# T and C of a state-space layer in one table, T's zero quarter not loaded, the input steps as outer partition index, and the transpositions put directly behind pv

## The chip, the cores and the metric

The kernel runs on one core of a Trainium2 chip. The metric is the device time of one launch in microseconds; of the kernel before, the median of three runs is 1155.27 us (1155.26 to 1155.54). The core has a matrix engine (TensorE, PE in the profile, its weight loads apart as PEld), a vector engine (VectorE, DVE), an activation engine (ScalarE, ACT), a general engine (GpSimd, POOL) and SyncE (SP), which in this kernel issues nearly all transfers. Every engine works through its own instructions in order and waits for others by semaphores. DMA engines carry the transfers.

## The reference

Two layers of width 1024 over 512 positions, float32. Layer 0 mixes with a stick-breaking attention, layer 1 with a complex diagonal state-space layer (SSM) and a GLU; each is followed by a gated MLP with a causal convolution of width 3, and everything is modulated by a vector c. The change concerns the SSM alone:

```python
def s5_ssm(h, w_in, a_re, a_im, log_dt, b_re, b_im, c_re, c_im, d_skip, w_glu, b_glu, w_o):
    u = h @ w_in
    ug = u.reshape(b, s, 64, 16)                     # 64 groups of 16 channels
    lam_bar = exp((a_re + 1j * a_im) * exp(log_dt)[:, None])   # 64 states a group
    b_bar = ((lam_bar - 1) / lam)[..., None] * (b_re + 1j * b_im)
    bu = einsum('gph,bsgh->bsgp', b_bar, ug)
    states = scan over s: x[s] = lam_bar * x[s - 1] + bu[s]
    y = einsum('ghp,bsgp->bsgh', c_re + 1j * c_im, states).real + d_skip * u
    z = gelu(y)
    return (z * sigmoid(z @ w_glu + b_glu)) @ w_o
```

## The kernel before, in words

Dense matrices are multiplied in three products of float32 halves (mm3, L170, L173, L174: high by high, high by low, low by high), each 128x128 against 128x512. A weight tile is loaded by SyncE (L162), its high half is made by ScalarE (L164) and its low half by VectorE (L165). In the background, wg tiles (L200, L201) carry the matrix-vector products with c.

The program runs in stages: attention, the first FFN (up and dn matmuls), the SSM, its GLU and output projection, the second FFN. The SSM's tables depend on weights alone, and they are made during the first FFN, from about 275 us of the profiled execution on, by ssm_prep.

**The tables.** The 64 groups are worked on in 8 blocks of 8 groups. The 512 positions are cut into 64 chunks of 8 steps. For each block there are four tables in device memory: B (input to the chunk's state contribution), R (rotations), T (the direct path, within a chunk, from 8 input steps x 16 channels to 8 output steps x 16 channels, for 8 groups) and C (from the chunk's starting state to the 8 output steps). T from input step j to output step i is zero where i < j.

**ssm_prep, per block.** GpSimd multiplies lam and bt (L1004 to L1009, called by cmul_in), with lam and bt loaded by load_bl (L1182, L1183; issued through held, which fixes SyncE's order and shows as L1173). SyncE stores lam to sB. GpSimd multiplies bc with powers to cl (L1232 to L1237). Then, for two blocks together (for block 7 alone), direct (L1161) lets TensorE multiply cl with bd to pk, from which ScalarE and VectorE write kz, a band of 112 zeros and 128 kernel values. t_out writes T out of kz: for input step j a window of 128 columns that begins at 112 - 16 j. cl_out writes C out of cl. The steps of ssm_prep are a generator whose pieces are put between the FFN's pieces, and its TensorE matmuls stand in the FFN's stream at places fixed by the program; held keeps the order of its transfers on SyncE, among weight loads.

**The SSM.** load_scan and load_out fetch B, R, T and C of a block, two blocks ahead. Per step s_, st_out(s_ - 2) multiplies u with T and the states with C into py (L1312 in the profile is the helper's line for py and pv; 8 matmuls each, shown as 16 of the trace's), st_scan(s_) multiplies u with B into pv and VectorE scans it; st_tr(s_ - 2) transposes yn, ScalarE's copy of py, into pz (L1396), and four gelus read pz. Dense glu matmuls fill TensorE between them: run(2) issues two of them between pv and the transpositions, run(100) the rest.

Of the kernel before, what the change touches and what calls it, by code (L numbers as in the profile page):

```python
# [8 lines left out]
F32 = mybir.dt.float32  # L9
# [8 lines left out]
P = 128  # L18
T = 512
D = 1024  # L20
KD = D // P
# [31 lines left out]
FINT = 1  # L53
FORD = (0, 1, 2, 3, 4, 5, 7, 6)
NGLU = 5
NU = 4
NPRE = 3
KPRE = 5
NWT = 6
# [26 lines left out]
def _trunk(ctx, tc, I, out, tap):  # L86
# [13 lines left out]
    dram = pool("dram", space=DRAM)  # L100
# [4 lines left out]
    def bank(p=None, name="ps"):  # L105
        p = p or mm
        return p.tile([P, 512], F32, tag="b", name=name)
# [32 lines left out]
    def follow(eng, fn):  # L140
        with tc.issue_after(line[eng].ins) if eng in line else ExitStack():
            line[eng] = fn()
        return line[eng]
# [837 lines left out]


    sB = dram.tile([8, P, 2, 512], F32, tag="sB", name="sB")
    sC = dram.tile([8, P, 8, P], F32, tag="sC", name="sC")
    sT = dram.tile([8, P, 8, P], F32, tag="sT", name="sT")
    sR = dram.tile([8, P, 2, 256], F32, tag="sR", name="sR")
    sL = dram.tile([2, 8, NPAIR * P], F32, tag="sL", name="sL")

# [2 lines left out]
    def ssm_prep(fc):  # L991
# [22 lines left out]
        def gen():  # L1014
# [152 lines left out]
            def t_out(bi, js):  # L1167
                kz = kza[:, bi % 2, :]
                for j in js:
                    held(sT[bi].rearrange("(h j) g c -> j g h c", j=8)[j], kz[:, 112 - 16 * j:240 - 16 * j])  # L1170

            def held(out, in_):
                tc.keep_in_program_order(SP.dma_start(out, in_))  # L1173


            def load_bl(bi):
                put = held if bi else G.dma_start
                lam = pb.tile([P, 2, 512], F32, tag="lam", name="lam")
                bt = pb.tile([P, 2, 512], F32, tag="bt", name="bt")
                cs = slice(bi * 512, (bi + 1) * 512)  # L1180
                for ri in range(2):
                    put(lam[:, ri, :], sL[ri, :, cs].rearrange("(o j) x -> o j x", o=1).to_broadcast([16, 8, 512]))  # L1182
                    put(bt[:, ri, :], I[("b_reT", "b_imT")[ri]][:, cs].rearrange("h (o x) -> h o x", o=1).to_broadcast([16, 8, 512]))  # L1183
                return lam, bt

            def cl_out(bi, cl):
                for ri in range(2):
                    for g2 in range(2):
                        held(sC[bi, ri * 64:ri * 64 + 64].rearrange("n (q g) c -> g n q c", g=2)[g2],
                             cl[g2 * 64:g2 * 64 + 64, ri, :, 1:, :].rearrange("n q a h -> n q (a h)"))  # L1190


# [78 lines left out]
    def ssm(R):  # L1271
# [3 lines left out]
        with ExitStack() as zc:  # L1275
# [3 lines left out]
            with ExitStack() as sc:  # L1279
                tp = sc.enter_context(tc.tile_pool(name="sst", bufs=1, reuse_waits="tile"))  # L1280

                def load_scan(bi):
# [3 lines left out]
                    for g, src in (("B", sB), ("R", sR)):  # L1286
                        follow("P", lambda: SP.dma_start(d[g].rearrange("p r n -> p (r n)"), src[bi].rearrange("p r n -> p (r n)")))

                def load_out(bi):
                    d = blk[bi]  # L1290
                    d["T"] = tp.tile([P, 8, P], F32, tag="pT", bufs=2, name="pT")
                    d["C"] = tp.tile([P, 8, P], F32, tag="pC", bufs=2, name="pC")
                    for g, src in (("T", sT), ("C", sC)):
                        follow("P", lambda: SP.dma_start(d[g].rearrange("p r n -> p (r n)"), src[bi].rearrange("p r n -> p (r n)")))

                for bi in range(2):
                    load_scan(bi)
# [9 lines left out]
                def run(n):  # L1307
                    for q in range(min(n, len(dense))):
                        dense.pop(0)()
# [5 lines left out]
                def u_out(bi, ps):  # L1315
                    d = blk[bi]
                    ut = sp.tile([P, CH, NC], F32, tag="ut", bufs=2, name="ut")
                    S.activation(ut, ps.rearrange("p (c j) -> p j c", j=CH), AF.Copy)
                    (S if bi < 4 else G).dma_start(sU[bi].rearrange("j p c -> p j c"), ut)
                    u = d["u"] = sp.tile([P, 8, NC], F32, tag="u", bufs=NU, name="u")  # L1320
                    pin["u"] = SP.dma_start(u.rearrange("p g c -> p (g c)"), sU[bi].rearrange("j (h g) c -> h j (g c)", g=8))

                for bi in range(4):
                    u_out(bi, hd[bi][1])
# [9 lines left out]
                def st_scan(bi):  # L1334
                    d = blk[bi]
                    u = d["u"]
                    rho = rhos[bi % 2]
                    S.activation(rho[:, :, 1:], decay[:, bi * 4:bi * 4 + 4].rearrange("p (q o) -> p q o", o=1).to_broadcast([P, 4, NC - 1]), AF.Copy)
                    pv = bank(aux, name=f"pv{bi}")
                    for q in range(4):  # L1340
                        for ri in range(2):
                            for g2 in range(2):
                                mm(pv[g2 * 64:g2 * 64 + 64, ri * 256 + q * 64:ri * 256 + q * 64 + 64],
                                   d["B"][:, ri, q * P + g2 * 64:q * P + g2 * 64 + 64], u[:, 2 * q + g2, :], start=True, stop=True)
                    R = d["R"]
                    v2 = pv.rearrange("p (r n) -> p r n", r=2)
                    cosb, sinb = (R[:, q:q + 1, :].to_broadcast([P, 2, 256]) for q in range(2))
                    rho = rho.rearrange("p q c -> p (q c)")

                    def tmp(tag, bufs=1):  # L1350
                        return sp.tile([P, 2, 256], F32, tag=tag, bufs=bufs, name=tag)

                    m1, m2, vr = tmp("m1", 2), tmp("m2"), tmp("vr")
                    V.tensor_tensor(m1, v2, cosb, ALU.mult)
                    V.tensor_tensor(m2, v2[:, ::-1, :], sinb, ALU.mult)
                    for ri in range(2):
                        V.tensor_tensor(m1[:, ri], m1[:, ri], m2[:, ri], (ALU.add, ALU.subtract)[ri])
                        V.tensor_tensor_scan(vr[:, ri], rho, m1[:, ri], 0.0, ALU.mult, ALU.add)
                    s1, s2 = tmp("m1", 2), tmp("m2")
                    V.tensor_tensor(s1, vr, cosb, ALU.mult)  # L1360
                    V.tensor_tensor(s2, vr[:, ::-1, :], sinb, ALU.mult)
                    for ri in range(2):
                        pin["comb"] = V.tensor_tensor(s1[:, ri], s1[:, ri], s2[:, ri], (ALU.subtract, ALU.add)[ri])

                    d["s1"] = s1
                    if not bi:
                        st_state(bi)
# [25 lines left out]
                def st_tr(bi):  # L1393
                    yn = blk[bi]["yn"]
                    for i in range(4):
                        pe_pin(PE.transpose(pz[:, i * P:(i + 1) * P], yn[:, 2 * i:2 * i + 2].rearrange("p i q h -> p (i q h)"), ident))  # L1396
                    for i in range(2):
                        for g2 in range(2):
                            S.activation(zf[bi][g2 * 64:g2 * 64 + 64].rearrange("p (a i c) -> p a i c", a=4, i=2)[:, :, i, :],
                                         pz[i * 64:i * 64 + 64].rearrange("p (a g c) -> p a g c", a=4, g=2)[:, :, g2, :], AF.Gelu_apprx_tanh)  # L1400
                    tap(f"z{bi}", zf[bi])
# [20 lines left out]
                def glu_w(mt):  # L1422
                    return load_w(I["w_glu"][(mt - NGLU) * P:(mt - NGLU + 1) * P, :], name=f"wgl{mt}")

# [9 lines left out]
                run(USTG[1])  # L1434
                pz = bank(name="pz")
                gb = None
                for s_ in range(2, 10):
                    st_out(s_ - 2)
                    if s_ < 8:
                        st_scan(s_)  # L1440
                    if s_ + 1 < 8:
                        load_scan(s_ + 1)
                    if s_ < 8:
                        load_out(s_)
                    if s_ > 2:
                        if s_ == 3:
                            zh = new_h()
                            gb = [bank(name=f"glu{mt}") for mt in range(NGLU)]
                        glu_units(s_ - 3)
                    run(2)  # L1450
                    st_tr(s_ - 2)
                    if s_ >= 8:
                        with behind_head([pin["low"], pin["comb"]]):
                            bg((1, 2)[s_ - 8], False)
                    run(100)

                gw, g5 = glu_w(NGLU), bank(aux, name=f"glu{NGLU}")
                for k in range(KD - 1):
                    mm3(g5, wk(gw, k), (zh[0][k], zh[1][k]), k == 0, False, True)
                glu_units(KD - 1)  # L1460
                run(100)
                mm3(g5, wk(gw, KD - 1), (zh[0][KD - 1], zh[1][KD - 1]), False, True, True)
                gb.append(g5)
            gp = zc.enter_context(tc.tile_pool(name="ssg", bufs=1, reuse_waits="tile"))
            gz = []
# [225 lines left out]
```

## Time and profile before

| | us |
|---|---|
| median of three runs | 1155.27 |
| profiled execution | 1157.38 |
| its span | 1155.6 |
| TensorE busy | 1145.3 (99%) |
| VectorE busy | 853.3 (74%) |
| ScalarE busy | 563.6 (49%) |
| GpSimd busy | 273.7 (24%) |

The profiled execution was 1157.38 us long, 2.1 us over the median; 1.8 us of it lie around the span. The mean granted TensorE clock is 0.998. Times of a timeline are us from the start of the span. An instruction's row gives its start, its length, engine, line, operation and tiles (out<-in), a count where several follow each other, and in brackets the idle time before it and what ended that. Matmuls overlap, so the distance of two starts is what a matmul costs, and less than its length.

### The profile page before, as it was taken

The numbers are of one execution on the slowest core, as the hardware profiler recorded it, in microseconds if no ns is written. First come the engines' busy times: TensorE is split into PE (matmuls) and PEld (weight loads), VectorE is DVE, ScalarE is ACT, GpSimd is POOL, SyncE is SP. The second block draws the span as 40 slices with busy tenths as digits, with TensorE's granted clock in tenths as the row PEclk, the third lists the DMA queues.
The fourth block names the chain that finished last, engine by engine and source line by source line (L and its number), as shares of the span: only waits on it lengthen the run. The fifth ranks groups of instructions, "written<-read, shape, count | busy, mean of one in ns | idle before, by whom it ended". The sixth has DMA issues, their size and how long they took to land.

```text
span 1155.6 us, 16407 instructions
## 1 busy us (share of the span) xinstructions
PE 1145.3 (99%) x6170; PEld 957.4 (83%) x6170; DVE 853.3 (74%) x1271; ACT 563.6 (49%) x894; POOL 273.7 (24%) x277
## 2 busy tenths in 40 slices
PE   9999999999999999999999999999999999999997
PEld 7888787798888888888889888899888888888887
DVE  7869989578987677777877688787886378744655
ACT  7656667456542244313446477547543144422443
POOL 1001010000678898779800000000000000000002
PEclk9999999999999999999999999999999999999999
DMA  9775564333367588697765797461366266332322
GB/s 345 282 264 162 183 201 147 126 92 110 94 207 245 157 267 247 192 311 251 233 219 192 225 333 278 167 201 56 110 218 200 73 159 207 126 111 75 93 69 73
DMA packets 87954, 211.00 MB, mean 183 GB/s; under 512 B 15554, under 2 KB 34114, under 8 KB 87875
## 3 DMA queue, kind: packets, MB, share of 16 engines
q1 hardware_dynamic: 79026, 192.39, 51.0%
q0 software_dynamic: 4544, 16.26, 4.3%
q10 hardware_dynamic: 4304, 1.31, 0.5%
q8 instruction: 48, 0.79, 0.3%
q14 instruction: 32, 0.25, 0.1%
HBM read 188.68 MB, written 21.24 MB: 182 GB/s over the span
## 4 chain that ended last, share of the span: by engine, by line
PE 92%; DMA 4%; DVE 2%; issue 1%; ACT 1%; SPq 0%; DVEq 0%
PE up L170 13%; PE up L173 13%; PE up L174 13%; PE dn L170 7%; PE dn L173 7%; PE dn L174 7%; PE up L333 4%; PE u L333 2%; PE o L838 1%; PE wo L170 1%; PE t L822 1%; PE wo L173 1%; PE wo L174 1%; PE wos L174 1%; PE wos L170 1%; PE wos L173 1%
## 5 line engine op out<-in xcount | busy, mean ns | idle before, releaser
L170 PE MATMUL up<-hH,up_h 128*128 128x512 f32 x640 | 249.6, 390 | 0.0
L173 PE MATMUL up<-hL,up_h 128*128 128x512 f32 x640 | 249.1, 389 | 0.0
L174 PE MATMUL up<-hH,up_l 128*128 128x512 f32 x640 | 249.0, 389 | 0.0
L461 DVE SCALAR_TENSOR_TENSOR ca<-up,small,ca 128x511 f32<-128x511 f32 (+1 forms) x176 | 131.6, 747 | 109.4 <-ACT ca L459 106.4
L170 PE MATMUL dn<-gH,dn_h 128*128 128x512 f32 (+1 forms) x394 | 144.5, 368 | 0.0
L173 PE MATMUL dn<-gL,dn_h 128*128 128x512 f32 (+1 forms) x394 | 144.4, 366 | 0.0
L174 PE MATMUL dn<-gH,dn_l 128*128 128x512 f32 (+1 forms) x394 | 144.3, 366 | 0.0
L170 PEld LDWEIGHTS up<-hH,up_h 128*128 128x128 f32 x640 | 120.1, 188 | 25.8 <-issue 0.4
L459 ACT ACTIVATE ca<-up,small 128x512 f32<-128x512 f32 x88 | 68.3, 776 | 149.3 <-PE up L174 143.2
L174 PEld LDWEIGHTS up<-hH,up_l 128*128 128x128 f32 x640 | 120.1, 188 | 25.0
L173 PEld LDWEIGHTS up<-hL,up_h 128*128 128x128 f32 x640 | 120.1, 188 | 24.7
L201 DVE SCALAR_TENSOR_TENSOR wg<-wg,cact 128x1024 f32<-128x1024 f32 x96 | 121.3, 1283 | 7.8 <-DMA wg<-in_w_modT_dram 7.7
L164 ACT ACTIVATE up_h<-up_r 128x1024 fp32r<-128x1024 f32 x80 | 84.2, 1052 | 83.2 <-PE dn L173 61.9
L165 DVE TENSOR_TENSOR up_l<-up_r,up_h 128x1024 fp32r<-128x1024 f32 x80 | 113.7, 1421 | 14.3 <-ACT up_h L164 13.4
L1554 POOL TENSOR_SCALAR xa<-x,Anorm_out 128x256 f32<-128x256 f32 x7 | 6.2, 881 | 461.4 <-DVE x L356 461.4
L356 DVE SCALAR_TENSOR_TENSOR x<-dn,mod,x 128x512 f32<-128x512 f32 (+1 forms) x55 | 37.4, 680 | 71.2 <-PE dn L174 71.2
L170 PEld LDWEIGHTS dn<-gH,dn_h 128*128 128x128 f32 x394 | 74.3, 189 | 12.4 <-issue 0.2
L173 PEld LDWEIGHTS dn<-gL,dn_h 128*128 128x128 f32 x394 | 74.3, 189 | 12.2
L174 PEld LDWEIGHTS dn<-gH,dn_l 128*128 128x128 f32 x394 | 74.3, 189 | 12.1
L164 ACT ACTIVATE dn_h<-dn_r 128x1024 fp32r<-128x1024 f32 (+1 forms) x48 | 46.5, 980 | 45.8 <-PE dn L173 40.8
L165 DVE TENSOR_TENSOR dn_l<-dn_r,dn_h 128x1024 fp32r<-128x1024 f32 (+1 forms) x48 | 61.3, 1278 | 2.4 <-ACT dn_h L164 2.1
L477 ACT ACTIVATE gH<-gm 128x512 fp32r<-128x512 f32 x44 | 27.1, 616 | 68.6 <-DVE gm L473 68.6
(356 smaller groups left out, 2276.8 us busy)
## 6 DMA issues: line engine op xcount, KB each, us to landing
up_r<-in_w_up_dram SPq DMA_DIRECT2D x80, 512.0 KB
wg<-in_w_modT_dram SPq DMA_DIRECT2D x74, 512.0 KB
dn_r<-in_w_down_dram SPq DMA_DIRECT2D x32, 512.0 KB
wg<-in_w_modT_dram POOLq DMA_DIRECT2D x22, 512.0 KB, 4.9
wgs<-in_w_modT_dram SPq DMA_DIRECT2D x16, 512.0 KB
dn_r<-in_w_down_dram SPq DMA_DIRECT2D x16, 384.0 KB
wv_r<-in_w_v_dram SPq DMA_DIRECT2D x8, 512.0 KB
wk_r<-in_w_qk_dram SPq DMA_DIRECT2D x8, 512.0 KB
```

Of the source, the lines that this page charges most:

```text
L164: order("S", lambda: S.activation(wh[:, :n], raw[:, :n], AF.Copy))
L165: pin["split"] = order("V", lambda: V.tensor_tensor(wl[:, :n], raw[:, :n], wh[:, :n].bitcast(F32), ALU.subtract))
L170: ins = PE.matmul(ps, ah, bh, start=start, stop=False)
L173: PE.matmul(ps, ah, bl, start=False, stop=False)
L174: PE.matmul(ps, al, bh, start=False, stop=stop)
L201: mul = lambda: V.scalar_tensor_tensor(w, w, 1.0, cact, ALU.mult, ALU.mult, accum_out=raw[:, col:col + 1])
L333: return pe_pin(PE.matmul(ps[:, cr], wk(w, k)[half], h[low][k][:, cr], start=k == 0 and cr.start == 0 and half + low == 0, stop=k == KD - ...
L356: add = lambda: V.scalar_tensor_tensor(xs, pv, gate, xs, ALU.mult, ALU.add)
L459: follow("S", lambda: S.activation(ca, ps, AF.Identity, bias=small[:, cb:cb + 1], scale=tapw[2]))
L461: follow("V", lambda: V.scalar_tensor_tensor(ca[:, q:], ps[:, :T - q], tapw[2 - q], ca[:, q:], ALU.mult, ALU.add))
L477: follow("S", lambda: S.activation(gh, m, AF.Copy))
L822: pe_pin(PE.transpose(pt[:, c:c + P], wts[pr][h2][i][:, j * P:(j + 1) * P], ident))
```

## The change: one table, another partition order, another place for the transpositions

T and C get one tile and one place in device memory (sT, 2 x 512 words of T and 1024 of C in each row). T's partitions are now (step, channel) where they were (channel, step), so that all entries from input steps 4 to 7 to output steps 0 to 3, which are zero, form a quarter of it: rows 64 to 127, columns 0 to 511. This quarter is set to zero once in each of the two tiles (GpSimd) and never loaded: load_out loads 64x512 and 128x1536. t_out writes T in halves of 64 columns (output steps 0 to 3, and 4 to 7), both for input steps 0 to 3, the second alone for 4 to 7. lam, bt and u follow the new partition order. In the SSM, the transpositions come directly behind pv, and the end of the loop is written out: py of block 7 earlier, and the dense group g5 in two pieces.

```diff
-    sC = dram.tile([8, P, 8, P], F32, tag="sC", name="sC")
-    sT = dram.tile([8, P, 8, P], F32, tag="sT", name="sT")
+    sT = dram.tile([8, P, 2 * TW + D], F32, tag="sT", name="sT")
...
             def t_out(bi, js):
                 kz = kza[:, bi % 2, :]
                 for j in js:
-                    held(sT[bi].rearrange("(h j) g c -> j g h c", j=8)[j], kz[:, 112 - 16 * j:240 - 16 * j])
+                    rows = sT[bi, j * 16:j * 16 + 16]
+                    for i in range(j // 4, 2):
+                        c0 = 112 - 16 * j + 64 * i
+                        held(rows[:, i * TW:(i + 1) * TW].rearrange("h (g c) -> g h c", g=8), kz[:, c0:c0 + 64])
...
-                    put(lam[:, ri, :], sL[ri, :, cs].rearrange("(o j) x -> o j x", o=1).to_broadcast([16, 8, 512]))
-                    put(bt[:, ri, :], I[("b_reT", "b_imT")[ri]][:, cs].rearrange("h (o x) -> h o x", o=1).to_broadcast([16, 8, 512]))
+                    put(lam[:, ri, :], sL[ri, :, cs].rearrange("j (o x) -> j o x", o=1).to_broadcast([8, 16, 512]))
+                    put(bt[:, ri, :], I[("b_reT", "b_imT")[ri]][:, cs].rearrange("(o h) x -> o h x", o=1).to_broadcast([8, 16, 512]))
...
+                tabs = [tp.tile([P, 2 * TW + D], F32, tag=f"tab{q}", name=f"tab{q}") for q in range(2)]
+                for t in tabs:
+                    G.memset(t[P // 2:, :TW], 0.0)
...
-                    for g, src in (("T", sT), ("C", sC)):
-                        follow("P", lambda: SP.dma_start(d[g].rearrange("p r n -> p (r n)"), src[bi].rearrange("p r n -> p (r n)")))
+                    for rows, cols in ((slice(0, P // 2), slice(0, TW)), (slice(0, P), slice(TW, 2 * TW + D))):
+                        follow("P", lambda: SP.dma_start(t[rows, cols], sT[bi, rows, cols]))
...
-                    pin["u"] = SP.dma_start(u.rearrange("p g c -> p (g c)"), sU[bi].rearrange("j (h g) c -> h j (g c)", g=8))
+                    pin["u"] = SP.dma_start(u.rearrange("p g c -> p (g c)"), sU[bi].rearrange("j (h g) c -> (j h) (g c)", g=8))
...
                     if s_ < 8:
                         st_scan(s_)
+                        st_tr(s_ - 2)
...
-                    run(2)
-                    st_tr(s_ - 2)
...
+                st_tr(6)
+                st_out(7)
                 gw, g5 = glu_w(NGLU), bank(aux, name=f"glu{NGLU}")
...
+                g5_units(range(G5K))
+                glu_units(6)
+                st_tr(7)
...
+                g5_units(range(G5K, KD - 1))
```

TensorE in the SSM, one step of the loop: before (py is the output of a block, pv the input of the scan, pz the transpositions, glu dense).

```order
L1312 MATMUL py_6706<-pC,st_6293 64x128 x8
L1312 MATMUL pv_6730<-u,pB 64x64 x16
L170 MATMUL glu_6670<-hH_6655,wglk_h 128x512
L173 MATMUL glu_6670<-hL_6663,wglk_h 128x512
L174 MATMUL glu_6670<-hH_6655,wglk_l 128x512
L170 MATMUL glu_6671<-hH_6655,wglk_h 128x512
L173 MATMUL glu_6671<-hL_6663,wglk_h 128x512
L174 MATMUL glu_6671<-hH_6655,wglk_l 128x512
L1396 MATMUL pz<-consts,yn 128x128 x4
L170 MATMUL glu_6672<-hH_6655,wglk_h 128x512
```

And with the change:

```order
L1321 MATMUL py_6733<-tab_6032,st_6324 64x128 x8
L1321 MATMUL pv_6757<-u,pB 64x64 x16
L1405 MATMUL pz<-consts,yn 128x128 x4
L172 MATMUL glu_6705<-hH_6690,wglk_h 128x512
L175 MATMUL glu_6705<-hL_6698,wglk_h 128x512
L176 MATMUL glu_6705<-hH_6690,wglk_l 128x512
```

The four transpositions stood behind six dense matmuls, and now stand between pv and the first of them.

TensorE in the first FFN, at pk of block 7 (up is the FFN's up projection): before.

```order
L174 MATMUL up_20_1_5481<-hH_2571,up_20_1_l 128x512
L1161 MATMUL pk_5558<-cl,bd 32x128 x8
L170 MATMUL up_21_0_5578<-hH_2564,up_21_0_h 128x512
```

With the change:

```order
L176 MATMUL up_20_1_5504<-hH_2570,up_20_1_l 128x512
L1162 MATMUL pk_5585<-cl,bd 32x128 x4
L172 MATMUL up_21_0_5609<-hH_2563,up_21_0_h 128x512
...
L176 MATMUL up_21_0_5609<-hH_2569,up_21_0_l 128x512
L1162 MATMUL pk_5585<-cl,bd 32x128 x4
L172 MATMUL up_21_0_5609<-hH_2570,up_21_0_h 128x512
```

The eight matmuls stood together; now four of them come 21 dense matmuls later.

SyncE in the first FFN, from the store of block 6's sB to the loads of block 7's bc: before.

```order
L1173 DMA sB<-lam 128x1024
L162 DMA up_20_1_r<-in_w_up_dram 128x1024
L1173 DMA sT<-kz 8x16x128 x4
L1173 DMA lam<-sL 128x1x512
...
L1173 DMA bt<-in_b_imT_dram 128x1x512
L1173 DMA sT<-kz 8x16x128 x4
...
L200 DMA wg_5421<-in_w_modT_dram 128x1024
L1173 DMA sT<-kz 8x16x128 x8
L1173 DMA sC<-cl 256x1x128 x4
L1173 DMA bc<-in_c_re_dram 128x64
```

With the change:

```order
L1177 DMA sB<-lam 128x1024
L164 DMA up_20_1_r<-in_w_up_dram 128x1024
L1177 DMA sT<-kz 8x16x64 x8
L1177 DMA lam<-sL 128x1x512
...
L1177 DMA bt<-in_b_imT_dram 128x1x512
L1177 DMA sT<-kz 8x16x64 x4
...
L202 DMA wg_5440<-in_w_modT_dram 128x1024
L1177 DMA sT<-kz 8x16x64 x12
L1177 DMA sT<-cl 64x4x128 x4
L1177 DMA bc<-in_c_re_dram 128x64
```

Ahead of lam there are eight stores of T where there were four, behind bt four as before, and ahead of C and bc twelve where there were eight. Blocks 5 and 6 have the same picture with eight and four.

More of the change, by code (lines that the diff above doesn't have):

```diff
@@ L55 @@
 NGLU = 5
+G5K = 3
 NU = 4
+TW = 512
 NPRE = 3
@@ L1188, in cl_out @@
                     for g2 in range(2):
-                        held(sC[bi, ri * 64:ri * 64 + 64].rearrange("n (q g) c -> g n q c", g=2)[g2],
+                        held(sT[bi, ri * 64:ri * 64 + 64, 2 * TW:].rearrange("n (q g c) -> g n q c", g=2, q=4)[g2],
                              cl[g2 * 64:g2 * 64 + 64, ri, :, 1:, :].rearrange("n q a h -> n q (a h)"))
@@ L1287, in load_scan @@
                         follow("P", lambda: SP.dma_start(d[g].rearrange("p r n -> p (r n)"), src[bi].rearrange("p r n -> p (r n)")))
+                tabs = [tp.tile([P, 2 * TW + D], F32, tag=f"tab{q}", name=f"tab{q}") for q in range(2)]
+                for t in tabs:
+                    G.memset(t[P // 2:, :TW], 0.0)
                 def load_out(bi):
                     d = blk[bi]
-                    d["T"] = tp.tile([P, 8, P], F32, tag="pT", bufs=2, name="pT")
-                    d["C"] = tp.tile([P, 8, P], F32, tag="pC", bufs=2, name="pC")
-                    for g, src in (("T", sT), ("C", sC)):
-                        follow("P", lambda: SP.dma_start(d[g].rearrange("p r n -> p (r n)"), src[bi].rearrange("p r n -> p (r n)")))
+                    t = tabs[bi % 2]
+                    d["T"] = t[:, :2 * TW].rearrange("p (i g c) -> p g i c", i=2, g=8)
+                    d["C"] = t[:, 2 * TW:].rearrange("p (g c) -> p g c", g=8)
+                    for rows, cols in ((slice(0, P // 2), slice(0, TW)), (slice(0, P), slice(TW, 2 * TW + D))):
+                        follow("P", lambda: SP.dma_start(t[rows, cols], sT[bi, rows, cols]))
                 for bi in range(2):
@@ L1436, in ssm @@
                 gb = None
-                for s_ in range(2, 10):
+                for s_ in range(2, 9):
                     st_out(s_ - 2)
@@ L1449, in ssm, with g5_units @@
                         glu_units(s_ - 3)
-                    run(2)
-                    st_tr(s_ - 2)
                     if s_ >= 8:
                         with behind_head([pin["low"], pin["comb"]]):
-                            bg((1, 2)[s_ - 8], False)
+                            bg(1, False)
                     run(100)
+                st_tr(6)
+                st_out(7)
                 gw, g5 = glu_w(NGLU), bank(aux, name=f"glu{NGLU}")
-                for k in range(KD - 1):
-                    mm3(g5, wk(gw, k), (zh[0][k], zh[1][k]), k == 0, False, True)
+                def g5_units(ks):
+                    for k in ks:
+                        mm3(g5, wk(gw, k), (zh[0][k], zh[1][k]), k == 0, k == KD - 1, True)
+                g5_units(range(G5K))
+                glu_units(6)
+                st_tr(7)
+                with behind_head([pin["low"], pin["comb"]]):
+                    bg(2, False)
+                run(100)
+                g5_units(range(G5K, KD - 1))
                 glu_units(KD - 1)
                 run(100)
-                mm3(g5, wk(gw, KD - 1), (zh[0][KD - 1], zh[1][KD - 1]), False, True, True)
+                g5_units(range(KD - 1, KD))
                 gb.append(g5)
```

## The prediction

> **What bounds the kernel now.** I read the page's first part and its chain, then a table of stretches, then the timelines of the two places that the change touches.
>
> ```profile
> PE 1145.3 (99%) x6170; PEld 957.4 (83%) x6170; DVE 853.3 (74%) x1271; ACT 563.6 (49%) x894; POOL 273.7 (24%) x277
> PE 92%; DMA 4%; DVE 2%; issue 1%; ACT 1%; SPq 0%; DVEq 0%
> ```
>
> TensorE is busy in 1145.3 of 1155.6 us, so only 10.3 us of idle time exist. A change gains where TensorE waits or pays for changing between kinds of matmul, and loses as soon as a new wait reaches it. No dense matmul is removed here.
>
> The first place is the SSM stage (columns: stretch, its length, then busy time and count of PE, PEld, DVE, ACT, POOL, granted clock, DMA share, GB/s):
>
> ```profile
> 680.00:695.00 15.00, 14.28 (x176) 12.01 (x174) 13.27 (x26) 10.60 (x25) 0.00 (x0) 1.00 1.04 339
> 695.00:710.00 15.00, 14.51 (x180) 12.23 (x176) 13.91 (x27) 10.36 (x23) 0.00 (x0) 1.00 0.88 333
> ```
>
> TensorE loses 0.72 and 0.49 us here while the DMA engines are full. Its timeline names where, and the chain of waits says behind what:
>
> ```profile
> 680.75 1.10 PE L1312 MATMUL pv<-u,pB 128*64 128x64 f32 x32
> 681.78 0.50 PE L170 MATMUL glu<-hH,wglk_h 128*128 128x512 f32 x1
> 682.12 0.40 PE L173 MATMUL glu<-hL,wglk_h 128*128 128x512 f32 x1
> 682.35 0.40 PE L174 MATMUL glu<-hH,wglk_l 128*128 128x512 f32 x1
> 683.28 0.60 PE L1396 MATMUL pz<-consts,yn 128*128 128x128 f32 x4
> 683.63 0.48 PE L170 MATMUL glu<-hH,wglk_h 128*128 128x512 f32 x1
> 683.95 0.39 PE L173 MATMUL glu<-hL,wglk_h 128*128 128x512 f32 x1
> 688.56 1.15 PE L1312 MATMUL pv<-u,pB 128*64 128x64 f32 x32 [0.72 <-DVE wglk_l L165]
> 696.19 1.15 PE L1312 MATMUL pv<-u,pB 128*64 128x64 f32 x32 [0.49 <-DMA pC<-sC]
> ...
> 680.09 10.13 DMA u<-sU
> ...
> 690.29 5.85 DMA pC<-sC
> ```
>
> pv reads u and pB, not wglk_l and not pC; a load from one full queue is what comes last both times.
>
> The second place is the preparation of the SSM tables during the first FFN. There TensorE has no gap at all (the table of 20 us stretches from 400 to 600 sums up to 200.00 of 200), but SyncE's queue and GpSimd form a loop that runs close to one TensorE instruction, pk of the last block:
>
> ```profile
> sum 200.00, PE 200.00 PEld 163.96 DVE 149.93 ACT 74.77 POOL 154.64; mean PE 20.00 PEld 16.40 DVE 14.99 ACT 7.48 POOL 15.46
> ...
> 516.54 2.27 POOL L1009 TENSOR_TENSOR lam<-bt,t 128x512 f32<-128x512 f32 x1
> 531.75 1.29 POOL L1004 TENSOR_TENSOR t<-lam,bt 128x512 f32<-128x512 f32 x1 [2.25 <-DMA lam<-sL]
> 540.95 1.29 POOL L1009 TENSOR_TENSOR lam<-bt,t 128x512 f32<-128x512 f32 x1
> 554.48 1.29 POOL L1004 TENSOR_TENSOR t<-lam,bt 128x512 f32<-128x512 f32 x1
> 562.82 2.27 POOL L1009 TENSOR_TENSOR lam<-bt,t 128x512 f32<-128x512 f32 x1
> 565.16 1.24 POOL L1232 TENSOR_TENSOR t<-bc,pw 128x576 f32<-128x576 f32 x1
> 567.66 2.30 POOL L1234 TENSOR_TENSOR cl<-t,t 128x576 f32<-128x576 f32 x1
> 573.39 2.03 POOL L1237 TENSOR_TENSOR cl<-t,t 128x576 f32<-128x576 f32 x1
> ...
> 575.38 0.64 PE L1161 MATMUL pk<-cl,bd 128*32 128x128 f32 x16
> ...
> 518.84 0.33 SPq L1173 DMA_DIRECT2D sB<-lam  x1
> 525.25 0.60 SPq L1173 DMA_DIRECT2D bt<-in_b_imT_dram  x1
> 542.27 0.33 SPq L1173 DMA_DIRECT2D sB<-lam  x1
> 543.52 2.52 SPq L1173 DMA_DIRECT2D sT<-kz  x4
> 546.13 0.58 SPq L1173 DMA_DIRECT2D lam<-sL  x1
> 552.66 0.33 SPq L200 DMA_DIRECT2D wg<-in_w_modT_dram  x1
> 553.47 5.66 SPq L1173 DMA_DIRECT2D sT<-kz  x8
> 561.81 0.61 SPq L1173 DMA_DIRECT2D bc<-in_c_re_dram  x1
> ```
>
> Round the loop: L1009 finishes lam, SyncE stores sB at once (540.95 + 1.29 = 542.24, sB at 542.27), issues the T stores, then the next block's lam and bt loads, and GpSimd waits for these (2.25 us at 531.75). At the end pk of block 7 starts at 575.38, while its last input, L1237, ends at 573.39 + 2.03 = 575.42: nothing in hand.
>
> **SSM stage, what the change gives.** T and C cost 2 x 512 = 1024 KB per block; now 64x512 and 128x1536 words, 128 + 768 = 896 KB. The 128 KB saved are 0.39 us at 339 GB/s. Two or three blocks of tables pass ahead of the two stalls, so loads behind them land 0.8 to 1.2 us earlier. The stalls are 0.72 + 0.49 = 1.21 us. Closed in full they give 1.2; if the 10.13 us of u's load is its own round trip, 0. I take 0.9, since the queue is full.
>
> The transposition: between dense matmuls the starts are 0.23 apart (682.12 to 682.35). pv to dense takes 0.34 (681.78 to 682.12), 0.11 more; pz to dense 0.32 (683.63 to 683.95), 0.09 more. With pz directly behind pv one such change falls away, 0.1 us a block, six blocks: 0.6 less. It would cost if pz had to wait for its yn:
>
> ```profile
> 680.97 0.60 ACT L1389 ACTIVATE yn<-py 128x512 f32<-128x512 f32 x1 [0.86 <-PE py L1312]
> ```
>
> yn ends at 681.57, and pv is issued until 681.78, so 0.2 us are in hand; that cover is thin, so I take 0.5 of the 0.6. The drain (g5 in two pieces, py of block 7 earlier) also moves one change or two: 0.1. The zero fills are two GpSimd memsets after its chain has ended at 575.42: nothing. The sum of this stage is -0.9 - 0.5 - 0.1 = -1.5 us, bounds -0.5 and -2.6 (stalls wholly gone, drain 0.4, the full 0.6 and 0.4 for loads behind the second stall).
>
> **Preparation, what the change costs.** T's stores become 96 where there were 64: for input steps 0 to 3 two DMAs each, so the first burst of each block goes from four to eight, ahead of the lam and bt loads on SyncE. Four took 2.52 us, so those loads are issued 2.5 us later. The second burst stays at four; at block 7 eight become twelve, ahead of sC and bc.
>
> Follow it from block 5 (L1004 at 508.31), ahead of which a wait of 8.47 us for bc soaks up whatever came late before:
>
> ```profile
> 494.76 1.22 POOL L1232 TENSOR_TENSOR t<-bc,pw 128x576 f32<-128x576 f32 x1 [8.47 <-DMA bc<-in_c_re_dram]
> 508.31 1.30 POOL L1004 TENSOR_TENSOR t<-lam,bt 128x512 f32<-128x512 f32 x1 [1.57 <-DMA lam<-sL]
> ...
> 504.77 0.54 SPq L1173 DMA_DIRECT2D bt<-in_b_imT_dram  x1
> ```
>
> Block 5 waits for lam already, so it is 2.5 late; its sB and the loads of block 6 behind it then are 2.5 + 2.5 = 5.0 late, and block 6 waited too (2.25), so 5.0 stays. The loads of block 7 are 7.5 late. GpSimd did not wait for them at 554.48; block 6's loads, issued by 525.85, were used at 531.75, 5.9 later, so block 7's (issued by 548.64) had at most 554.48 and perhaps 551.6, as block 5's (issued by 505.31) took 3.0. Block 7's L1004 is thus 4.9 to 7.5 late. bc of block 7 stands behind four further stores: 7.5 + 2.5 = 10.0 late, less 0.9 us of gaps in SyncE's rows around 552.66: 9.1. It was there by 565.16 at the latest and issued at 561.81. So cl of block 7 comes 7 to 9 us late; I take 8.
>
> On top, lam and bt are now loaded with the 8 input steps as the outer index, where it was 16. Stretches with little but sT stores (outer 8) against stretches of lam and bt loads (outer 16):
>
> ```profile
> 469.20:470.00 0.80, 0.80 (x6) 0.65 (x5) 0.39 (x2) 0.80 (x2) 0.72 (x2) 1.00 0.50 146
> 527.60:529.60 2.00, 2.00 (x10) 1.65 (x10) 0.62 (x1) 0.00 (x0) 1.90 (x1) 1.00 0.99 285
> ```
>
> The former fill half of the DMA engines. One block's lam and bt are 4 x 256 KB = 1.05 MB: 3.7 us at 285 GB/s, 7.2 at 146, so up to 3.5 us a block; the lower bound is nothing, since the issue alone (four of 0.6) takes 2.5. Over blocks 5 to 7 I add 1.5, nearer the lower bound because pieces of 2 KB should move better than sT's of 512 B: cl is 9.5 us late.
>
> What waits is pk, and all dense matmuls behind it on TensorE. In the order of the change its first half stays, needs L1234 (567.66 + 2.30 = 569.96) and so has 5.4 us in hand; the second half comes 21 dense matmuls later, 21 x 0.23 = 4.8 us, so it has as much less the first half's wait. The stall is 9.5 - 5.1 = 4.4 us, once. The extra visit to pk costs 0.2 (two changes). Bounds of the stall: 0, if cl is under 5 late, and 8.8, with 1.5 us more in each of three blocks. Stores, weights and wg behind on SyncE come later as well, but TensorE's 200.00 of 200 says that the weight tiles keep ahead of it; I put that at nothing, and if that cover is gone each us costs one.
>
> **Sum.** +0.2 + 4.4 - 1.5 = +3.1 us. The profiled execution took 1157.38, 2.1 over the median of 1155.27; I set the sum on the median: 1158.4.
>
> **Rivals.**
> *Lateness is absorbed.* The planner's places leave more room than I read, or bc and lam land early: cl is under 5 us late, pk does not wait, and -1.5 + 0.2 = -1.3 stays: 1154.0. For it: block 7's L1004 did not wait at all. Against: blocks 5 and 6 did.
> *The other side, faster.* The same, with the SSM's bound in full: every load lands ahead of pv, six changes of 0.1 gone, no extra visit felt: -2.4, 1152.9. It decides from 1.2 us of earlier landing, what three blocks give at 339 GB/s. Against it, the 10.13 us of u.
> *Half the DMA engines.* lam and bt with outer index 8 move at 146 GB/s: 8.8 + 0.2 - 1.5 = +7.5, 1162.8. For it, the two stretches above; against it, those stores have other pieces, and the issue may hide it.
> The Trainium skill, "DMA: Bandwidth & Descriptors", section "Rules for kernel authors", says that an outermost dimension of c < 16, such as a leading repeated one, keeps the whole transfer on at most c engines. By that rule this rival is the likelier form of the loss; this trace agrees for the sT stores (share 0.50) and has no load of that form.
> *The joined table makes py wait.* py's first eight matmuls need T alone before, and now all of a 768 KB transfer with C in it. C landed only at 696.14 (690.29 + 5.85). Eight matmuls, 0.45 us, move behind that in three blocks: +1.3, less 0.5 of the changes, plus 0.2: 1156.3.
>
> **Chances.** Forecast 0.50, absorbed 0.27, faster in full 0.08, half engines 0.10, joined table 0.05. What can be told from no change here is 0.2%, 2.3 us: 1152.96 to 1157.58. The forecast's own range is 1156 to 1162, and about 0.11 of its 0.50 lies under 1157.58. Faster: 0.08 and 0.06 of the absorbed case, 0.14. Same: 0.21 + 0.11 + 0.05 = 0.37. Slower: 0.39 + 0.10 = 0.49. The range goes from 1153.2 to 1162.8: below lie the 0.08 and some 0.05 of the absorbed case, above half of the half-engine case and little of the forecast, 0.2 together.
>
> **What would show it.** In the profile after, pk of block 7 with a wait on cl and TensorE under 20.00 in the stretch 560:580 or 580:600; L1004 of blocks 5 to 7 with longer waits for lam and bt; T stores in eights ahead of them; the stretch of lam and bt loads with a share near 0.5 if the half-engine step holds. In the SSM, pv without the two gaps, pz starting within 0.3 us after pv's end, and fewer GB. I am wrong if pk(7) starts within 1 us of its dense neighbours, or if weight loads behind the stores become TensorE's wait.

## The result, and the profile after

The changed kernel takes 1175.63 us (median of six runs, 1168.81 to 1178.92), the kernel before, run beside it, 1155.49 (1155.26 to 1155.89): the ratio is 1.0169, 95% interval 1.0153 to 1.0185, 20 us slower. The prediction had the side, slower, but 1158.4 us and a range that ends at 1162.8. The runs of the changed kernel also lie 10 us apart, where those of the kernel before lie within 0.6; only one of them was profiled, so what sets a run's place in these 10 us is open.

The profiled execution of the changed kernel took 1178.91 us, 3.3 over its median; its span is 1177.1 us, 21.5 more than the one before. Its waits of TensorE (engine, line, what it waited for, then total us, times, longest; dn is the FFN's down projection, gH and gL are the halves of its input). The change and the runs below move line numbers by a few: L1004 of the kernel before is L1005 here, L1161 is L1162, L1232 is L1236.

```profile
PE pk L1162 <- POOL cl L1238: 11.5, 1, 11.5
PE pk L1162 <- POOL cl L1241: 3.6, 2, 3.3
PE dn L176 <- DVE dn_l L167: 1.1, 1, 1.1
...
PE stat L283 <- DVE acc L251: 0.7, 1, 0.7
PE dn L172 <- DVE x L358: 0.6, 1, 0.6
PE dn L175 <- DVE gL L480: 0.6, 1, 0.6
PE dn L172 <- ACT gH L479: 0.5, 1, 0.5
```

The two rows of pv are gone, and pk waits for cl, as the prediction said, but 15.1 us instead of 4.4, and not only in block 7: 3.3 us are at 547.71, where pk of blocks 4 and 5 waits. The other five rows, 3.5 us, are new as well; one of them is for a weight half, dn_l.

After such waits TensorE is slow for a while. The two long waits, and stretches of 10 us around them (columns as in the prediction; the number ahead of the DMA share is the granted clock):

```profile
547.71 0.43 PE L1162 MATMUL pk<-cl,bd 128*32 128x128 f32 x8 [3.27 <-POOL cl L1241]
...
595.50 0.66 PE L1162 MATMUL pk<-cl,bd 128*32 128x128 f32 x8 [11.52 <-POOL cl L1238]
```

```profile
540.00:550.00 10.00, 6.73 (x54) 5.03 (x53) 9.86 (x12) 3.52 (x5) 7.42 (x5) 0.92 0.53 155
550.00:560.00 10.00, 10.00 (x41) 8.10 (x40) 2.88 (x4) 2.93 (x4) 8.37 (x6) 0.91 0.98 300
...
580.00:590.00 10.00, 3.98 (x18) 2.97 (x16) 7.98 (x11) 4.62 (x7) 4.89 (x4) 0.80 0.40 93
590.00:600.00 10.00, 4.50 (x18) 3.35 (x19) 5.85 (x8) 3.36 (x5) 8.18 (x6) 0.52 0.75 223
```

The missing clock costs time only where TensorE works. Behind the first wait the starts of dense matmuls are 0.43 us apart from 548.40 to 551.80, instead of 0.23, and TensorE works all that time: (0.08 + 0.09) x 10 = 1.7 us. Ahead of the second wait, until 583.98, they are still 0.23 apart, so the clock missing in 580:590 falls into the wait and costs nothing; behind it, from 595.50 to about 599.6, 4.1 us run at half the clock: 2.1 us. Together an estimate of 3.8 us. So the sum of the loss is 15.1 (pk) + 3.5 (other waits) + 3.8 (clock) = 22.4. Against it stands the SSM, by the first and the last pv of each kernel, before and then after:

```profile
L1312 PE MATMUL pv<-u,pB x256: 219/222/270, 652.3 to 704.0; 128*64 128x64 f32 x128
```

```profile
L1321 PE MATMUL pv<-u,pB x256: 219/222/270, 676.3 to 726.1; 128*64 128x64 f32 x128
```

51.7 us became 49.8: 1.9 us less. 22.4 - 1.9 and the 0.2 that was forecast for pk's second visit are 20.7 of the 21.5 us; 0.8 stays unexplained.

Where cl comes so late from is seen on GpSimd. Three starts of the lam product in the kernel before (blocks 1, 2 and 4):

```profile
412.56 1.28 POOL L1004 TENSOR_TENSOR t<-lam,bt 128x512 f32<-128x512 f32 x1 [0.41 <-DMA lam<-sL]
434.50 1.29 POOL L1004 TENSOR_TENSOR t<-lam,bt 128x512 f32<-128x512 f32 x1 [1.70 <-DMA lam<-sL]
...
476.53 1.29 POOL L1004 TENSOR_TENSOR t<-lam,bt 128x512 f32<-128x512 f32 x1 [0.44 <-DMA lam<-sL]
```

and after, with the bc product of block 4, the lam product of block 7 and the bc product of block 7 behind them:

```profile
417.75 1.29 POOL L1005 TENSOR_TENSOR t<-lam,bt 128x512 f32<-128x512 f32 x1 [4.17 <-DMA lam<-sL]
443.68 1.29 POOL L1005 TENSOR_TENSOR t<-lam,bt 128x512 f32<-128x512 f32 x1 [4.97 <-DMA lam<-sL]
494.61 1.29 POOL L1005 TENSOR_TENSOR t<-lam,bt 128x512 f32<-128x512 f32 x1 [6.12 <-DMA lam<-sL]
505.03 2.08 POOL L1236 TENSOR_TENSOR t<-bc,pw 128x576 f32<-128x576 f32 x1
575.93 1.29 POOL L1005 TENSOR_TENSOR t<-lam,bt 128x512 f32<-128x512 f32 x1 [3.53 <-DMA lam<-sL]
591.59 1.21 POOL L1236 TENSOR_TENSOR t<-bc,pw 128x576 f32<-128x576 f32 x1 [6.62 <-DMA bc<-in_c_re_dram]
```

Blocks 1 and 2 are 5.2 and 9.2 us late, and no store of T stands ahead of their loads on SyncE (the first of them is issued at 454.03): the loads themselves have become slower. Block 4 is 18.1 late; the gap before its bc product swallows 8 of that (505.03 against 494.76 leaves 10.3), and by block 7 it is 21.5 and, for bc, 26.4 us.

### The profile page after: what moved, and what is told of

It reads as the page before. It is cut to its first block, busy times and chain, and to the rows that moved or that the text cites. A ratio compares the mean times of both kernels' runs of the same rounds, so it can differ in the third digit from the quotient of the medians.

```text
span 1177.1 us, 16425 instructions
## 1 busy us (share of the span) xinstructions
PE 1150.1 (98%) x6170; PEld 959.6 (82%) x6170; DVE 853.6 (73%) x1271; ACT 562.6 (48%) x894; POOL 273.3 (23%) x279
## 4 chain that ended last, share of the span: by engine, by line
PE 68%; DMA 12%; POOL 9%; DVE 5%; SPq 4%; issue 2%; ACT 1%; DVEq 0%; POOLq 0%; ACTq 0%
PE up L172 6%; PE up L175 6%; PE up L176 6%; PE up L335 4%; PE dn L176 4%; PE dn L175 4%; PE dn L172 4%; SPq L1177 3%; DMA lam<-sL 3%; DMA up_r<-in_w_up_dram 3%; PE u L335 2%; PE o L840 2%; PE t L824 2%; PE wo L172 1%; DMA wg<-in_w_modT_dram 1%
## 5 line engine op out<-in xcount | busy, mean ns | idle before, releaser
L175 PEld LDWEIGHTS up<-hL,up_h 128*128 128x128 f32 x640 | 120.9, 189 | 25.2
L203 DVE SCALAR_TENSOR_TENSOR wg<-wg,cact 128x1024 f32<-128x1024 f32 x96 | 122.3, 1293 | 18.2 <-DMA wg<-in_w_modT_dram 18.1
```

The costliest lines, as they stand in the source:

```text
L175: PE.matmul(ps, ah, bl, start=False, stop=False)
L203: mul = lambda: V.scalar_tensor_tensor(w, w, 1.0, cact, ALU.mult, ALU.mult, accum_out=raw[:, col:col + 1])
```

## The experiments

My theory after this: the lam and bt loads, with 8 input steps as the outer index of their source, run on half of the DMA engines, in every block; the 32 further stores of T on SyncE are the smaller part. The rival: the stores are the cause, and the loads are late because they stand behind them. Four runs take the change apart. (The planner in what follows is the step of the build that fixes each engine's order of instructions.)

**Partition order alone.** The kernel before with the new order of lam, bt, u and T's rows; 64 stores of T, T and C loaded whole. TensorE's order of instructions is that of the kernel before, and SyncE's too but for one C load a place later.

```diff
-put(lam[:, ri, :], sL[...].rearrange("(o j) x -> o j x", o=1).to_broadcast([16, 8, 512]))
+put(lam[:, ri, :], sL[...].rearrange("j (o x) -> j o x", o=1).to_broadcast([8, 16, 512]))
 (bt the same way)
-held(sT[bi].rearrange("(h j) g c -> j g h c", j=8)[j], ...)
+held(sT[bi].rearrange("(j h) g c -> j g h c", j=8)[j], ...)
```

> The kernel before with the new partition order alone (step outside, channel inside, for lam, bt, u and T's rows); T is stored in 64 transfers and loaded whole as before. Theory A (the lam and bt loads with 8 as outer index run on half the DMA engines, in every block from the first on): each block's lam lands 3 to 5 us later, a part is soaked up at block 4, pk of block 7 waits 10 to 16 us, 1165 to 1173 us. Rival B (the further T stores on SyncE are the cause): no wait, 1155 to 1156 us.

Measured: 1167.47 us (1165.65 to 1169.11), ratio 1.0105 (1.0089 to 1.0120). Its waits:

```profile
PE pk L1161 <- POOL cl L1234: 5.1, 1, 5.1
PE pk L1161 <- POOL cl L1237: 3.9, 1, 3.9
```

12 us, as theory A had it, with the same stores in number and place. (The wait, 9.0 us, is a little under the 10 to 16 expected; TensorE's clock was 0.52 from 580 to 590 on top.) The rows of T's stores are new here too; that the loads alone make the difference is shown by the run with repaired loads below. A stretch of this run in which little but lam and bt loads move, and two such of the changed kernel below it:

```profile
408.50:409.70 1.20, 1.20 (x7) 0.97 (x7) 0.83 (x1) 1.20 (x3) 1.20 (x2) 1.00 0.53 157
```

```profile
462.50:465.50 3.00, 3.00 (x15) 2.49 (x14) 2.72 (x4) 0.64 (x1) 2.92 (x2) 1.00 0.51 158
519.00:522.00 3.00, 3.00 (x15) 2.49 (x14) 1.10 (x2) 0.00 (x0) 1.73 (x1) 1.00 0.48 147
```

In the kernel before the same loads had a share of 0.99 and 285 GB/s; now it is about half, at 147 to 158 GB/s. Busy time and rate fell together: 285 / 0.99 = 288, 158 / 0.51 = 310 GB/s per full share. So a busy DMA engine moves bytes as fast as before, and half of the engines' time is idle; had the engines themselves been slowed, by reading the same rows one behind the other for instance, the share would have stayed full at a lower rate. The Trainium skill, "DMA: Bandwidth & Descriptors", "Rules for kernel authors", says just that of an outermost dimension under 16; this trace agrees, 0.5 of 16 for an outer 8.

**Stores alone.** The kernel before with 96 stores of T in the old order, lam and bt as before:

```diff
-held(sT[bi].rearrange("(h j) g c -> j g h c", j=8)[j], kz[:, 112 - 16 * j:240 - 16 * j])
+rows = sT[bi].rearrange("(h j) g c -> j g h c", j=8)[j]
+if j < 4:
+    for i in range(2):
+        c0 = 112 - 16 * j + 64 * i
+        held(rows[:, :, 64 * i:64 * i + 64], kz[:, c0:c0 + 64])
+else:
+    held(rows, kz[:, 112 - 16 * j:240 - 16 * j])
```

> The kernel before with T stored in 96 transfers instead of 64 (8 and 4 per block, 12 at the end), old partition order, lam and bt loaded as before. Theory A: what my prediction had without its slower loads, cl of block 7 7 to 9 us late, pk of block 7 (split here too) waits 2 to 4 us, 1157 to 1160 us. Rival B (the stores make the loss): 1170 us or more. If GpSimd's room is larger than I read: 1155 to 1156 us.

Measured: 1158.24 us (1157.57 to 1160.65), ratio 1.0028 (1.0016 to 1.0040): 2.7 us. The planner splits pk of block 7 in this kernel too, so the split comes from the stores. In the profile cl of block 7 is 5.4 us late (its last product ends at 578.79 + 2.03 = 580.82, before at 575.42), where I had 8. The rows are the lam products of blocks 6 and 7, the bc product and the last product of block 7, then TensorE's waits:

```profile
533.73 1.29 POOL L1004 TENSOR_TENSOR t<-lam,bt 128x512 f32<-128x512 f32 x1 [3.80 <-DMA lam<-sL]
555.93 1.83 POOL L1004 TENSOR_TENSOR t<-lam,bt 128x512 f32<-128x512 f32 x1 [0.40 <-DMA lam<-sL]
571.72 1.23 POOL L1238 TENSOR_TENSOR t<-bc,pw 128x576 f32<-128x576 f32 x1 [5.59 <-DMA bc<-in_c_re_dram]
578.79 2.03 POOL L1243 TENSOR_TENSOR cl<-t,t 128x576 f32<-128x576 f32 x1
...
PE dn L170 <- DVE x L356: 2.1, 1, 2.1
...
PE pk L1161 <- POOL cl L1240: 0.8, 1, 0.8
```

The time is in the range expected, but not for the reason given. The stores do not make the loop later and later: the lam products of blocks 6 and 7 are 2.0 and 1.5 us late (531.75 and 554.48 before), where I had 5.0 and 4.9 to 7.5. pk waits 0.8 us instead of 2 to 4, and the down projection, which I had put at nothing, 2.1. That the price came out near is in part luck; this profile, too, is of a run 2.4 us over its kernel's median.

**The loads repaired.** The change, with the same loads in the same places, but from sources that hold the rows twice (lam; one further transfer fills them) and eight times (bt, laid out so by the host), so that the outer index is 16 and 128:

```diff
-sL[ri, :, cs].rearrange("j (o x) -> j o x", o=1).to_broadcast([8, 16, 512])
+sL2[ri, :, cs].rearrange("j (o x) -> j o x", o=1).to_broadcast([16, 8, 512])
-I["b_reT"][:, cs].rearrange("(o h) x -> o h x", o=1).to_broadcast([8, 16, 512])
+I["b_reT"][:, cs]                                   # laid out with 128 rows
 (b_imT the same way)
```

> The change, with lam and bt loaded from copies that have 16 or 128 as the outer index (lam's source holds each row twice, bt's source eight times; the same number of loads, the same 2 KB pieces). Theory A: lam lands as before, only the stores' lateness is left, 1155.5 to 1158.5 us, with the SSM's gain of 1 to 1.5 us in it. Rival B: 1170 to 1176 us as the change.

Measured: 1158.30 us (1156.71 to 1162.04), ratio 1.0030 (1.0017 to 1.0043). 17.3 of the 20 us are gone with the outer index alone, and the 2.8 that stay are about what the stores alone cost, as theory A had it. Of TensorE's waits for cl one is left (in a profile of a run 3.1 us over the median):

```profile
PE pk L1164 <- POOL cl L1240: 2.6, 1, 2.6
```

The two parts are not additive: 12.0 + 2.7 = 14.7 us alone, 20.1 together. My reading is that lateness is soaked up once (the 8 us at block 4) and that what comes on top counts in full, with the clock's loss behind longer waits; no run tests this.

**The SSM loop alone.** The kernel before with the transpositions directly behind pv and the drain written out, nothing else:

```diff
     if s_ < 8:
         st_scan(s_)
+        st_tr(s_ - 2)
...
-    run(2)
-    st_tr(s_ - 2)
```

> The kernel before with the SSM loop of the change alone (transpositions directly behind pv, drain written out); tables, order and stores as before. By the prediction's terms 0.5 for six changes between kinds of matmul and 0.1 for the drain: 1154.9 us, bounds 1154.2 to 1155.4. If pz waits for yn behind pv: 1155.5 to 1157 us.

Measured: 1155.56 us (1154.66 to 1156.64), ratio 1.0000 (0.9991 to 1.0009): no difference, where 1154.9 was expected. In its profile, the slowest of its eleven runs, the SSM stretch is 49.8 us against 51.7, but pk of block 7 waited:

```profile
PE pk L1162 <- POOL cl L1238: 1.3, 1, 1.3
```

This kernel's preparation is the old one, and the profile of the kernel before has no such wait. So it seems to come and go by itself: the prediction's "nothing in hand" is a place where the kernel before, too, stands at the edge. To see the loop without it, block 7's bc loads were put ahead of its stores on SyncE, with the loop and, as a control, without:

```diff
+if bi == 7:
+    bc = load_bc()
     t_next()
```

> The kernel before with the SSM loop of the change, and with block 7's two bc loads put ahead of its eight T stores and four C stores on SyncE, so that cl of block 7 has 5 us and more in hand. The run with the loop alone saved 2.0 us between the first and the last pv, but pk of block 7 waited 1.3 us there and its time was that of before. Theory C (the wait at pk hid the gain): 1153.5 to 1154.5 us, no wait at pk. Rival D (the gain is no gain over many runs, or goes elsewhere): 1155.3 to 1155.8 us.

> The kernel before with the bc loads of block 7 ahead of the stores alone. If pk of block 7 waits now and then in the kernel before as well: 0.3 to 1 us less, 1154.5 to 1155.2 us. If it never waits there: 1155.5 us as before.

Measured: with the loop 1155.00 us (1154.42 to 1155.73), ratio 0.9994 (0.9985 to 1.0003); the control 1155.71 (1154.63 to 1157.49), ratio 1.0000 (0.9991 to 1.0009), beside 1155.70 for the kernel before. By the medians the loop is worth 0.7 us, and the interval does not exclude nothing. The time lies between theory C, which had 1.2 to 2.2 us, and rival D; the control is where it was expected if pk never waits. From pv to pv in the control's timeline (two steps between the rows), and then with the new loop:

```profile
680.79 1.10 PE L1318 MATMUL pv<-u,pB 128*64 128x64 f32 x32
...
694.65 1.10 PE L1318 MATMUL pv<-u,pB 128*64 128x64 f32 x32
```

```profile
680.00 1.10 PE L1319 MATMUL pv<-u,pB 128*64 128x64 f32 x32
...
693.72 1.10 PE L1319 MATMUL pv<-u,pB 128*64 128x64 f32 x32
```

6.93 against 6.86 us a block, 0.07 (I had 0.1); and the control, whose SSM is that of the kernel before, has neither of the two stalls at pv. They were in the profiled execution of the kernel before, which was 2.1 us over the median. The two other profiles with the old loop bear this out: the one with the order alone has no wait at pv, the one with the stores alone a single one of 0.4 us. So the stalls come and go, and most of the 1.9 us that the SSM stretch lost is not the loop's: it is 50.1 us in the control, 49.8 with the new loop. What made the stalls was not tried.

**The stores moved.** Does the rest of the loss go when T's stores get out of the way? Twice the bursts were exchanged (four stores ahead of lam, eight behind) with block 7's bc ahead, once with the loads repaired and once without:

```diff
-ts += [(q, range(4)), (q, range(4, 8))]
+ts += [(q, range(4, 8)), (q, range(4))]
```

> The change with lam and bt loaded with 16 outside (as in the run that repaired the loads), the second burst of T stores (four) put ahead of the lam and bt loads and the first (eight) behind them, and block 7's bc ahead of its stores. If the stores' place is what was left of the loss: pk of block 7 no longer waits, the SSM's 2 us remain, 1153.3 to 1154.5 us. If not: 1157 to 1159 us.

> The change with the two bursts of T stores exchanged and bc of block 7 ahead, lam and bt still loaded with 8 outside. If the two causes add up, the stores' part (about 2.8 us alone, more where the loop is already late) goes and the loads' part stays: 1164 to 1170 us. If the loads only hurt together with the stores: under 1160 us.

Measured: with the repaired loads 1162.37 us (1161.62 to 1164.20), ratio 1.0058 (1.0046 to 1.0071); without 1177.41 (1175.66 to 1180.90), ratio 1.0188 (1.0168 to 1.0208). Both are misses. With the loads repaired pk waits no more, as expected, but the time is worse by 4 us than without the exchange; TensorE's waits and SyncE's timeline in that run:

```profile
PE dn L172 <- ACT dn_h L166: 2.9, 1, 2.9
PE dn L172 <- ACT gH L479: 2.4, 1, 2.4
...
572.74 9.43 SPq L1179 DMA_DIRECT2D sT<-kz  x12
582.26 2.61 SPq L1179 DMA_DIRECT2D sT<-cl  x4
584.97 7.39 SPq L1179 DMA_DIRECT2D sT<-kz  x12
592.41 0.93 SPq L164 DMA_DIRECT2D dn_r<-in_w_down_dram  x2
```

The planner has put the last 12 stores ahead of two down weights that stood before them in the run with repaired loads; these now leave 19.7 us after 572.74, and the projection waits for them. In the run without the repair the stores stand in the same place, dn waits 6.2 us for gH, and pk still waits 10.7. The wait had moved to another instruction, or come on top. So the last stores, 24 of them, were given to GpSimd's queue, which is free by then, once with the tables and once (16 stores) without:

```diff
 def t_out(bi, js):
+    held = held_g if bi > 5 else held_sp      # GpSimd for blocks 6 and 7, SyncE for the others
```

> The run with repaired loads, exchanged bursts and bc ahead had no wait at pk left, but waited 2.9 and 2.4 us for down weights, whose loads stood behind 36 T stores on SyncE. Here the last 24 of these (blocks 6 and 7) are issued by GpSimd, which has nothing else to do by then. If the pile of stores ahead of the down weights was the rest of the loss: 1154 to 1155 us, no wait at dn. If the tables still cost elsewhere: over 1156 us.

> The kernel before with the SSM loop of the change, block 7's bc ahead of its stores, and the last 16 T stores (blocks 6 and 7) issued by GpSimd: the same without the joined tables and with the old partition order. 1154.4 to 1155.2 us. The difference to the run with the tables is what the tables (128 KB less per block, against 96 stores and the new order) are worth once nothing of the preparation waits: by the prediction's terms up to 0.9 us, by the SSM stretch of the runs so far (48.9 us with the new loop alone, from the first pv to the last) nothing.

Measured: with the tables 1155.87 us (1154.81 to 1157.02), ratio 1.0001 (0.9992 to 1.0010); without them 1155.16 (1154.61 to 1155.74), ratio 0.9994 (0.9985 to 1.0003). With the tables 6.5 us came back against the run before, and no wait at dn is left: there the pile of stores ahead of the down weights was the loss. The time lies between the two cases expected. And the tables show no gain: the steps of pv are 6.86 us in both, with 128 KB less per block or without. The tables' kernel is 0.7 us the slower by the medians, so a small cost may be left: in its profile, the slowest of eleven, pk waits 1.4 us again, in the other not at all.

## Why the prediction was wrong

The path was right: the loop of SyncE and GpSimd falls behind, cl of block 7 comes late, pk waits, and all dense matmuls stand behind it. What makes it late was weighed the wrong way round: 8 of the 9.5 us of lateness were put down to the stores and 1.5 to the loads. cl came 25.2 us late and pk waited 15.1 us instead of 4.4, by these terms:

- **"Over blocks 5 to 7 I add 1.5."** This is the step that failed: it puts the slower loads at 1.5 us of lateness, where the order alone, which has them and not one store more, cost 12.0 us of time; 17.3 of the change's 20 go when the loads are repaired. I had the row that says half the engines (0.50, 146 GB/s) and the price of it (3.5 us a block), and took a value near the lower end because the pieces are larger and the issue takes 2.5 us anyway. The larger pieces did not help: 0.48 to 0.53 and 147 to 158 GB/s for pieces of 2 KB, beside 0.50 and 146 for sT's of 512 B. And the issue does not hide it, since SyncE itself waits for earlier transfers to land before it issues later ones. Its waits after, between 380 and 620 us, and then three pieces of the chain that leads to the wait of 11.5 us (start, length, what):

```profile
SPq L1177 <- DMA lam<-sL: 9.4, 5, 2.9
SPq L1177 <- DMA bt<-in_b_imT_dram: 8.1, 6, 1.5
...
SPq L164 <- DMA lam<-sL: 3.5, 3, 2.5
SPq L202 <- DMA lam<-sL: 2.7, 1, 2.7
```

```profile
567.79 7.98 DMA lam<-sL
...
575.79 7.59 DMA wg<-in_w_modT_dram
...
589.17 2.28 DMA bc<-in_c_re_dram
```

  23.7 us in these four rows alone. Before, the same view has 2.3 for bt and 1.3 and 0.8 for lam. A slow load is thus paid twice, by GpSimd that waits for it and by the queue behind it: in the chain SyncE issues wg when lam has landed (567.79 + 7.98 = 575.77), issues the later ones of T's twelve stores when wg has landed (575.79 + 7.59 = 583.38), and reaches bc at 589.17.
- **"A wait of 8.47 us for bc soaks up whatever came late before."** It soaks up 8, but 18.1 came, and block 4 still left 10.3 us late. I counted the stores there and forgot that the loads of blocks 1 to 4 have the new form too.
- **The stall, L - 5.1.** The formula holds for the stores alone only roughly (cl 5.4 late, 0.8 at pk), and in the change cl is some 25 late. From what the prediction says ahead of it the two halves' waits add up to L - 4.8, not L - 5.1; that is 0.3 us. The term for TensorE's clock after a stall, about 3.8 us, was not in the sum.
- **"Stores, weights and wg behind on SyncE ... I put that at nothing."** 3.5 us in the change, 2.1 with the stores alone; the run with exchanged bursts shows that this cover is as thin as that of pk.
- **The SSM, -1.5.** The sum was near what the two profiles show (-1.9), but for a wrong reason. The 0.9 for earlier loads rests on two stalls of one execution, which the control did not have, so the agreement is luck. The 0.5 for changes between kinds of matmul is 0.07 a block, some 0.4 in all, the only part that stayed.

The rival "half the DMA engines" was the right case. It had a chance of 0.10, and even its price, 1162.8, was too low. It counted the slower loads in three blocks only, and there with 2 us a block, though the rows had given 3.5: with that, three blocks alone are 8 + 3 x 3.5 - 5.1 + 0.2 - 1.5 = 12.1 us, 1167.4. The rule of the Trainium skill beside it was the stronger evidence for it, and the prediction said so without giving it the chance. The joined table made no wait at py: no row of py stands among TensorE's waits. Of what was to be seen, L1004's longer waits, the stores in eights and the share near 0.5 all came, and of the signs of being wrong a part, the wait at dn for a weight half.

## What to carry to other kernels

When an edit turns the partition order of a tile round, look at what its loads have as outermost index, for every transfer that fills it and not only for the one that the edit is about: here 16 to 8 there cost 12 us, and the 128 KB per block that were saved somewhere else gave nothing that the runs show, while the further stores for it cost 2.7. Where a row of the profile already shows transfers with the new outer index, take its rate and do not discount it for a difference that was not measured; and follow a loop over several engines from its first round, not from the round where it last had room. A stall in one profiled execution that lies over the median is not yet a stall of the median; look for it in a second profile before a gain is counted on it.

## What the runs showed of the hardware

- Loads with an outer index of 8 had a DMA share of 0.48 to 0.53 for up to 3 us in which little else moved, at 147 to 158 GB/s; with 16 it was 0.99 and 285.
- Within and behind the 11.5 us in which TensorE waited, the granted clock was 0.80 and 0.52 in two stretches of 10 us, and 0.52 in the run with the order alone as well; about 3.8 us of the loss of the change, by the estimate above. The Trainium skill, "TensorE: Matmul & The Clock Gate", Part 1, "The HAM clock gate", gives half rate after an idle window of about 3.4 us; these rows agree with it (0.52). But shorter waits did it too: behind the 3.27 us at 547.71 matmuls started 0.43 us apart for 3.4 us, and the waits of 2.6 us with the repaired loads (clock 0.52 from 577.5 to 581) and of 2.1 us with the stores alone (0.69 from 615 to 620) were followed by a stretch at half clock as well, so in these traces 2.1 us were enough. Behind the 1.3 us with the loop alone and the 1.4 us of the run with GpSimd's stores there is none.
- One visit to the transpositions between dense matmuls costs 0.07 us a block more than directly behind pv.
